# Delta rule: the inverse's products with z and with the z-part of k v made for all chunks at once, and wide norms by GpSimd's power

## Chip, cores and metric

One core of one Trainium2 chip runs one launch. The metric is the device time of that launch in microseconds; the median of three runs of the kernel before is 3610.85 us (3596.32 to 3610.88).

## The reference, cut to what matters

Three layers over 2048 tokens of width 1024: sliding window attention, a gated recurrence (HGRN2), and a hybrid of gated linear attention and the RWKV-7 delta rule, each between norms. What the change touches most is the delta rule, per head of 64 and per token:

```
sa = jnp.einsum('bhvk,bhk->bhv', S, -kk_t)
S = (S * w_t[:, :, None, :]
     + sa[..., None] * (kk_t * a_t)[:, :, None, :]
     + v_t[..., None] * k_t[:, :, None, :])
y = jnp.einsum('bhvk,bhk->bhv', S, r_t)
```

There are 8 such heads. The other touched piece is `lax.rsqrt(mean + eps)` of the norms: per head of 128 in the recurrence and in the linear attention, per head of 64 behind the delta rule.

## The kernel before, in words

The tokens are taken in four phases of 512. Matrix products of the layers (`ch`, `ch_two`, `unit_tok`) run in float32r as three products of 128-row high and low parts: `hth` and `htl` are activations, `wp` weights, `psA` and `psB` the PSUM banks of this main stream. Heads are worked on beside it in float32: `hgrn_head` and `gla_pair` with `gate_out`, and `delta_pair`.

`delta()` walks through the delta rule as one thread: four phases, and in each four pairs of heads, 16 calls of `delta_pair` in all. A pair's 512 tokens are 8 chunks of 64. Phase by phase a pair needs columns `u` that the main stream writes to DRAM. In a pair:
- products of decayed k, b with z and r give the masked blocks `AS`; the part that is to be inverted goes to DRAM (`md`, 4 transfers) and comes back as `Mb` (lines 1775 to 1805);
- 31 pairs of VectorE operations (`pr`, `X`, lines 1839 to 1841) invert 32 by 32 blocks; `X` goes to DRAM (`xd`, 4 transfers) and comes back as `XB` (1844 to 1849); two rounds of 32 by 32 products (`psV`, `psX`) complete the inverse `Xt`, 64 by 64 for each chunk and head;
- `psU` (1826 to 1835) is what z takes from k v, put into the upper half of `VV`, whose lower half is v;
- the recurrence (1885 to 1909) runs over the 8 chunks: `psQ` is the product of z and r with the state `Sbd`; VectorE adds `VV` (`P1`, tile `P`); TensorE multiplies by the inverse (`psQ<-P,Xt`); ScalarE copies the result into `VV`; TensorE makes the state's increment `psSt` and completes the output in `psQ` (`psQ<-VV,AS`); VectorE updates `Sbd`; ScalarE copies the output to `y`;
- norm, gate and a transfer of the pair's output, on which the last layer's out product (`F`) waits.

`rsqrt` (537) makes a norm's factor. For one column a GpSimd power does it; for 4 columns (`gate_out`, 1414: 48 calls) and 8 (`delta_pair`, 1919: 16 calls) VectorE makes it with a bit shift and three Newton steps, 11 operations on tiles `rsi` and `rst` behind the first.

The order of instructions on each engine is written out ahead. `Threads` interleaves the generators by an estimate of time; each instruction is recorded with its cost and what it depends on (`Pace.record`, 261), and `Pace.order` (314) simulates the five queues (the SP queue issues every transfer) and fixes the order in each. While the main stream is on TensorE, side work is let in when it has been ready for 1 us, and then all that is ready together. The last pair is moved ahead in priority (line 1668). `record` takes a DRAM tensor's access as one interval, so the four `xd` writes, which interleave, count as depending on one another in this plan. The planner's price for a GpSimd power is line 243:

```
            return 0.4 + n * 0.165
```

PSUM banks of `delta_pair` come from `psb`, two of them; SBUF buffers from `dbig`, 16.

Of the kernel before, what the change touches and what calls it, by code (L numbers as in the profile page):

```python
# [11 lines left out]
F32 = mybir.dt.float32  # L12
F32R = mybir.dt.float32r
BF16 = mybir.dt.bfloat16
I32 = mybir.dt.int32
AF = mybir.ActivationFunctionType
ALU = mybir.AluOpType
AX = mybir.AxisListType
PSUM = bass.MemoryType.PSUM
DRAM = bass.MemoryType.DRAM  # L20

P = 128
# [122 lines left out]
class Pace:  # L145
# [115 lines left out]
    def record(self, ins, eng, op, outs, ins_, rest, priority):  # L261

        n, deps = len(self.log), set()
        inside = lambda a, b: a[0] >= b[0] and a[1] <= b[1] and a[2] >= b[2] and a[3] <= b[3] and not b[4]
        for x in outs + ins_:
            name = x.tensor.name
            if self.follows.get(name):
                deps.add(self.first[self.follows[name]])
            self.first.setdefault(name, n)
        for x in ins_:  # L270
            key, area = self.area(x)
            w, r = self.uses.setdefault(key, [[], []])
            deps.update(i for a, i in w if x.space == "PSUM" or self.meet(a, area))
            if x.space == "PSUM":
                deps.update(i for _, i in r if self.log[i][1] != eng)
        for x in ins_:
            key, area = self.area(x)
            self.uses[key][1].append((area, n))
        for x in outs:
            key, area = self.area(x)  # L280
            u = self.uses.setdefault(key, [[], []])
            for k in range(2):
                deps.update(i for a, i in u[k] if i != n and (x.space == "PSUM" or self.meet(a, area)))
                u[k][:] = [v for v in u[k] if v[1] == n or not inside(v[0], area)]
            u[0].append((area, n))
        table = next((self.TABLES[f] for f in rest if f in self.TABLES), None) if eng == "act" else None
        mode = None
        if eng == "pe":
            rows, cols = ins_[0].shape[0], math.prod(ins_[0].shape[1:])
            if op == "transpose":  # L290
                cols = P
            mode = *(32 if k <= 32 else 64 if k <= 64 else P for k in (rows, cols)), "r" if ins_[0].dtype == F32R else "t" if op == "transpose" else "f"
        if eng == "dma" and any(s != 1 or k <= 256 for x in (outs[0], ins_[0]) for s, k in x.ap[-1:]):
            self.short.add(n)
        saved, self.table = self.table, table[0] if table else self.table
        cost = self.cost(eng, op, outs, ins_, rest)
        self.table = saved
        self.begin.append(self.at["pe"] if eng == "dma" and self.at["pe"] < 80.0 else 0.0)
        self.log.append((ins, eng, cost, deps, priority, table, mode))
# [191 lines left out]
def rec_stack(ctx: ExitStack, tc: tile.TileContext, A, out, T=2048, layers=(0, 1, 2)):  # L491
    nc = tc.nc
    NPH = T // TQ
    pace = Pace(tc)
    te, ve, se, ge, sy = (pace.engine(e, n) for e, n in (
        (nc.tensor, "pe"), (nc.vector, "dve"), (nc.scalar, "act"), (nc.gpsimd, "pool"), (nc.sync, "dma")))
# [5 lines left out]
    mx = ctx.enter_context(tc.tile_pool(name="mx", bufs=1))  # L502
    turn = Turns(mx, 1, pace)
    sm = Turns(ctx.enter_context(tc.tile_pool(name="sm", bufs=4)), 4, pace)
# [6 lines left out]
    yrow = Buffers(mx, "y", 4, pace)  # L511
    mrg = Buffers(mx, "g", 8, pace)
    big = Buffers(mx, "a", 13, pace)
    dbig = Buffers(mx, "b", 16, pace)
    psd = Buffers(psp, "d", 2, pace)
    psm = Buffers(psp, "m", 4, pace)
    psb = Buffers(psp, "e", 2, pace)

    def need(ev):
        if ev not in done:  # L520
            yield ev

    def bank(pool, name, ahead=0):
        return pool.take([P, TQ], F32, name, ahead=ahead)
# [12 lines left out]
    def rsqrt(dst, src, scale, eps, n):  # L537

        ve.tensor_scalar(dst, src, scale, eps, ALU.mult, ALU.add)
        if n == 1:  # L540
            ge.tensor_tensor(dst, dst, mhalf, ALU.pow)
            return

        i = sm.tile([P, 8], I32, tag="rsi", name="rsi")[:, :n]
        t = sm.tile([P, 8], F32, tag="rst", name="rst")[:, :n]
        y = i.bitcast(F32)
        ve.tensor_scalar(i, dst.bitcast(I32), 1, None, ALU.logical_shift_right)
        ve.tensor_scalar(i, i, -1, 0x5f3759df, ALU.mult, ALU.add)
        for k in range(3):
            ve.tensor_tensor(t, y, dst, ALU.mult)  # L550
            ve.scalar_tensor_tensor(t, t, -0.5, y, ALU.mult, ALU.mult)
            ve.scalar_tensor_tensor(y if k < 2 else dst, t, 1.5, y, ALU.add, ALU.mult)


    def w_ch(w, *cols):
# [145 lines left out]
    H2 = [slice(0, 64), slice(64, 128)]  # L701
# [22 lines left out]
    def row_stat(x, name, rstd=None):  # L724
        ss = sm.tile([P, 1], F32, tag="ss" + name, name="ss" + name)
        se.activation(out=junk, in_=x, func=AF.Square, accum_out=ss)
        if rstd is None:
            rstd = sm.tile([P, 1], F32, tag="rstd" + name, name="rstd" + name)
        rsqrt(rstd, ss, 1.0 / D, EPS, 1)
        return rstd  # L730
# [160 lines left out]
    ident = cst.tile([P, P], F32, name="ident")  # L891
    junk = cst.tile([P, D], BF16, name="junk")
    mhalf = cst.tile([P, 1], F32, name="mhalf")
# [779 lines left out]
    def delta_pair(ph, hp, wa):  # L1673
# [4 lines left out]
        def new(name, shape=(P, TQ), dt=F32):  # L1678
            return dbig.take(list(shape), dt, name)
# [5 lines left out]
        for n in (hp, 4 + hp, 8 + hp):  # L1685
            yield from need(("u", n, ph))
            t = yield from new("u")
            sy.dma_start(out=t, in_=ud[n, ph])
            src.append(t)
        r, k, v = src  # L1690
# [5 lines left out]
        ps = yield from bank(psb, "psW")  # L1696
# [5 lines left out]
        ps = yield from bank(psb, "psAa")  # L1702
# [14 lines left out]
        ps = yield from bank(psb, "psN")  # L1717
# [19 lines left out]
        ZR, BK = [], []  # L1737
# [19 lines left out]
        AS = [[None, None], [None, None]]  # L1757
        for h in range(2):
# [4 lines left out]
            for c in range(4):  # L1763
                for n in range(2):
                    te.matmul(pn[n][:, P * c:P * c + P], lhsT=BK[h][H2[n], c].rearrange("p f t -> p (f t)"),
                              rhs=ZR[h][H2[n], c].rearrange("p f t -> p (f t)"), start=True, stop=True)
# [24 lines left out]
        ps = yield from bank(psb, "psVT")  # L1791
# [4 lines left out]
        VV = []  # L1796
# [10 lines left out]
        ps = yield from bank(psb, "psBo")  # L1807
# [6 lines left out]
        BKt = []  # L1814
        for h in range(2):
            ps = yield from bank(psb, "psBK")
# [6 lines left out]
            psb.give(ps)  # L1823
        dbig.give(*BKh)

        for h in range(2):
            ps = yield from bank(psb, "psU")
            for c in range(4):
                for n in range(2):
                    te.matmul(ps[0:64, P * c + 64 * n:P * c + 64 * n + 64], lhsT=AS[n][h][64:128, 0, c],  # L1830
                              rhs=VV[h][64:128, c, 64 * n:64 * n + 64], start=True, stop=True)
                yield
            yield
            se.copy(VV[h][0:64].rearrange("p c d -> p (c d)"), ps[0:64])
            psb.give(ps)
# [14 lines left out]
        Xt = []  # L1850
# [10 lines left out]
        ps = yield from bank(psb, "psV2")  # L1861
        for m in range(16):
            c, n = divmod(m, 2)
# [6 lines left out]
        ps = yield from bank(psb, "psX")  # L1870
# [6 lines left out]
            se.copy(Xt[h][0:32, :, 32:64], ps[0:32, 256 * h:256 * h + 256].rearrange("p (m t) -> p m t", m=8))  # L1877
        psb.give(ps)

        gate = yield from new("gate")  # L1880
        yield from need(("u", 13 + hp, ph))
        sy.dma_start(out=gate, in_=ud[13 + hp, ph])
        y = yield from new("y", (P, 4, P))
        yield
        for c in range(8):
            h, cc = divmod(c, 4)
            pq = yield from bank(psb, "psQ")
            te.matmul(pq[:, 0:P], lhsT=ZR[h][:, cc].rearrange("p f t -> p (f t)"), rhs=Sbd, start=True, stop=True)
            yield
            P1 = sm.tile([64, P], F32, tag="P1", bufs=1, name="P1")  # L1890
            ve.tensor_tensor(P1, pq[0:64, 0:P], VV[h][0:64, cc], ALU.add)
            yield
            for n in range(2):
                te.matmul(pq[0:64, P + 64 * n:P + 64 * n + 64], lhsT=Xt[h][:, 2 * cc + n], rhs=P1[:, H2[n]], start=True, stop=True)
            yield
            se.copy(VV[h][0:64, cc], pq[0:64, P:2 * P])
            yield
            pst = yield from bank(psb, "psSt")
            for n in range(2):
                te.matmul(pst[H2[n], 0:64], lhsT=BKt[h][:, cc, n], rhs=VV[h][:, cc, H2[n]], start=True, stop=True)  # L1900
            for n in range(2):
                te.matmul(pq[64:128, H2[n]], lhsT=AS[n][h][:, 1, cc], rhs=VV[h][:, cc, H2[n]], start=False, stop=True, skip_group_check=True)
            yield
            for n in range(2):
                ve.scalar_tensor_tensor(Sbd[H2[n], H2[n]], Sbd[H2[n], H2[n]], WC[H2[n], c], pst[H2[n], 0:64], ALU.mult, ALU.add)
            psb.give(pst)
            yield
            se.copy(y[H2[c % 2], c // 2], pq[64:128, 0:P])
            psb.give(pq)
        dbig.give(*ZR, *VV, *Xt, *BKt, *AS[0], *AS[1])  # L1910

        mv = sm.tile([P, 8, 2], F32, tag="mv", name="mv")
        for i in range(4):
# [12 lines left out]
        ps = yield from bank(psb, "psYT")  # L1926
# [26 lines left out]
    for i, (kind, ph) in enumerate(order):  # L1953
        head, body, tail, chains, n = build[kind](i, ph, seq)
# [88 lines left out]
```

## Time and profile before

| | |
|---|---|
| median of three runs | 3610.85 us |
| the profiled execution | 3609.73 us |
| its span, first to last instruction | 3607.9 us |
| TensorE matmul busy | 3418.6 us, 95% |
| VectorE busy | 2395.9 us, 66% |
| ScalarE busy | 1298.1 us, 36% |
| GpSimd busy | 438.6 us, 12% |
| transfers in flight, share of 16 engines | 55% |
| mean granted TensorE clock | 0.976 |

The profiled execution lies 1.9 us above its span and 1.1 us under the median. Every recorded operation has the same source line (the helper that emits it), so rows are told apart by their tiles. A float32 product appears as two matmul instructions, a transpose and a float32r product as one.

### The profile page before, as it was taken

Reading aid. Unit: us, or ns where it says so; the run is one execution under the profiler, and the core shown is the slowest. Engines: PE = TensorE matmul, PEld = TensorE weight load, DVE = VectorE, ACT = ScalarE, POOL = GpSimd, SP = SyncE. Lnnn points to the kernel's source line nnn. Section 1 sums busy time; section 2 is a strip of 40 time slices with the busy share of each in tenths; the row PEclk is TensorE's granted clock in tenths of the full one; section 3 lists DMA queues with packets and bytes.
Section 4 is the critical chain, followed back from the end, with each engine's and each line's share of the span. In section 5 each row is a group of like instructions: output and inputs, shape, how many; then the busy total and the mean of one; then the engine's idle time right before and its main releaser. Section 6 shows DMA issues by size and latency. Waiting matters only on the chain.

```text
span 3607.9 us, 76010 instructions
## 1 busy us (share of the span) xinstructions
PE 3418.6 (95%) x30488; PEld 2929.9 (81%) x30488; DVE 2395.9 (66%) x6735; ACT 1298.1 (36%) x3379; POOL 438.6 (12%) x649
## 2 busy tenths in 40 slices
PE   4999999999999999999999999999999999999997
PEld 4788888888878788878787787888888787888886
DVE  4777666567675876986747758665766766566574
ACT  3655433345433232454222324422232332333232
POOL 2321135410150000000000002300000000011000
PEclk8999999999999999999999999999999999999998
DMA  7666567755586344444754345675344366455663
GB/s 192 184 205 220 172 228 237 235 178 192 208 276 215 128 130 147 148 164 166 246 200 133 123 142 166 238 257 172 122 141 156 110 239 236 155 176 164 233 226 128
DMA packets 351105, 666.35 MB, mean 185 GB/s; under 512 B 164640, under 2 KB 246560, under 8 KB 298016
## 3 DMA queue, kind: packets, MB, share of 16 engines
q1 hardware_dynamic: 350752, 661.49, 55.1%
q8 instruction: 240, 3.93, 0.4%
q14 instruction: 113, 0.93, 0.1%
HBM read 494.42 MB, written 166.99 MB: 183 GB/s over the span
## 4 chain that ended last, share of the span: by engine, by line
PE 68%; DVE 21%; DMA 5%; ACT 3%; issue 2%; SPq 1%; POOL 0%; DVEq 0%; ACTq 0%; POOLq 0%
PE psA L431 29%; PE psB L431 18%; DVE pr L431 4%; PE psO L431 4%; PE psQ L431 3%; DVE X L431 3%; PE psL L431 2%; PE psPT L431 2%; PE psS L431 2%; DVE y L431 1%; SPq L431 1%; DVE AS L431 1%; DMA wp<-wk 1%; PE psT L431 1%; PE psKV L431 1%
## 5 line engine op out<-in xcount | busy, mean ns | idle before, releaser
L431 PE MATMUL psA<-hth,wp 128*128 128x512 f32 (+1 forms) x5120 | 1477.1, 367 | 65.3 <-ACT qs L431 27.4
L431 PEld LDWEIGHTS psA<-hth,wp 128*128 128x128 f32 x5120 | 914.7, 192 | 221.1 <-ACT qs L431 27.8
L431 PE MATMUL psA<-htl,wp 128*128 128x512 f32 (+1 forms) x2560 | 934.9, 366 | 0.0
L431 PE MATMUL psB<-wp,mgh 128*128 128x256 f32 x3072 | 579.5, 286 | 9.2 <-DVE y L431 3.4
L431 PEld LDWEIGHTS psA<-htl,wp 128*128 128x128 f32 x2560 | 490.8, 192 | 68.8 <-issue 5.3
L431 PEld LDWEIGHTS psB<-wp,mgh 128*128 128x128 f32 x3072 | 480.8, 190 | 20.5 <-issue 4.9
L431 POOL TENSOR_TENSOR wp<-wf,wp 128x256 fp32r<-128x256 f32 x412 | 344.5, 868 | 897.2 <-ACT wp L431 890.1
L431 PE MATMUL psB<-wp,mgl 128*128 128x256 f32 x1536 | 440.5, 287 | 3.4 <-DVE mgl L431 3.4
L431 PE MATMUL psB<-wp,hth 128*128 128x256 f32 x1536 | 300.3, 291 | 4.6 <-DMA wp<-wk 2.3
L431 PEld LDWEIGHTS psB<-wp,mgl 128*128 128x128 f32 x1536 | 291.1, 190 | 7.8 <-DVE mgl L431 5.1
L431 PEld LDWEIGHTS psB<-wp,hth 128*128 128x128 f32 x1536 | 245.5, 193 | 10.5 <-DMA wp<-wk 2.8
L431 PE MATMUL psB<-wp,htl 128*128 128x256 f32 x768 | 222.8, 290 | 0.0
L431 DVE TENSOR_TENSOR pr<-X,Mb 128x16 f32<-128x16 f32 (+30 forms) x496 | 207.1, 417 | 10.9
L431 DVE TENSOR_TENSOR y<-psB,y 128x256 f32<-128x256 f32 x256 | 97.2, 418 | 123.3 <-PE psB L431 122.6
L431 DVE SCALAR_TENSOR_TENSOR Sbd<-Sbd,WC,psSt 64x64 f32<-64x64 f32 x256 | 71.4, 279 | 161.0 <-PE psSt L431 157.8
L431 POOL MEMSET Xt<- 32x256 f32 x32 | 9.7, 304 | 1197.1 <-PE psM L431 891.7
L431 DVE TENSOR_REDUCE X<-pr 128x8 f32<-128x16 f32 (+30 forms) x496 | 146.0, 294 | 11.2
L431 ACT ACTIVATE junk<-y 128x1024 bf16<-128x1024 f32 (+1 forms) x128 | 94.4, 737 | 161.6 <-DVE y L431 149.4
L431 PEld LDWEIGHTS psB<-wp,htl 128*128 128x128 f32 x768 | 148.5, 193 | 3.0 <-issue 1.5
L431 ACT CAST wp<-wf 128x1024 fp32r<-128x1024 f32 x103 | 108.0, 1049 | 112.6 <-PE psB L431 49.4
L431 ACT ACTIVATE S<-S,nm 128x257 f32<-128x257 f32 (+1 forms) x256 | 126.8, 498 | 56.9 <-DVE nm L431 54.3
L431 ACT COPY VV<-psQ 64x128 f32<-64x128 f32 x128 | 33.1, 259 | 244.3 <-PE psQ L431 242.6
(283 smaller groups left out, 5457.2 us busy)
## 6 DMA issues: line engine op xcount, KB each, us to landing
wp<-wk SPq DMA_DIRECT2D x309, 1024.0 KB, 5.1
wk<-wp SPq DMA_DIRECT2D x103, 1024.0 KB, 5.3
xin<-x SPq DMA_DIRECT2D x48, 512.0 KB, 5.1
wf<-in_rec_w_in_dram SPq DMA_DIRECT2D x32, 512.0 KB, 6.8
x<-y SPq DMA_DIRECT2D x32, 512.0 KB, 3.6
wf<-in_w_in_dram SPq DMA_DIRECT2D x29, 512.0 KB, 6.6
ud<-um SPq DMA_DIRECT2D x52, 256.0 KB, 4.2
u<-ud SPq DMA_DIRECT2D x48, 256.0 KB, 3.4
```

The source lines that it names most:

```text
L431: r = f(*a, **k)
```

## The change

- In `delta_pair`, z of each chunk is transposed on TensorE by a product with the identity (`Zt`, two banks, a ScalarE copy each), ahead of `psU`.
- When `Xt` is complete, 16 products of 64 by 64 (`psXZ`) put the inverse times z where z stood in `ZR`, and 16 more (`psXU`, two banks) put the inverse times what z takes from k v where that stood in `VV`; ScalarE copies, two for `psXZ` and one for each bank of `psXU`.
- In the recurrence the product with `Xt` and ScalarE's copy are gone: VectorE's addition writes `VV` itself.
- `dbig` has 18 buffers in place of 16.
- `rsqrt` is a GpSimd power for any number of columns.
- In the planner, a write to a DRAM tensor depends on earlier reads of it alone, no longer on earlier writes.

```
-            for k in range(2):
+            for k in range(1 if x.space == "DRAM" else 0, 2):
                 deps.update(i for a, i in u[k] if i != n and (x.space == "PSUM" or self.meet(a, area)))
-                u[k][:] = [v for v in u[k] if v[1] == n or not inside(v[0], area)]
+                if x.space != "DRAM":
+                    u[k][:] = [v for v in u[k] if v[1] == n or not inside(v[0], area)]
...
-    dbig = Buffers(mx, "b", 16, pace)
+    dbig = Buffers(mx, "b", 18, pace)
...
         ve.tensor_scalar(dst, src, scale, eps, ALU.mult, ALU.add)
-        if n == 1:
-            ge.tensor_tensor(dst, dst, mhalf, ALU.pow)
-            return
-
-        i = sm.tile([P, 8], I32, tag="rsi", name="rsi")[:, :n]
-        t = sm.tile([P, 8], F32, tag="rst", name="rst")[:, :n]
-        y = i.bitcast(F32)
-        ve.tensor_scalar(i, dst.bitcast(I32), 1, None, ALU.logical_shift_right)
-        ve.tensor_scalar(i, i, -1, 0x5f3759df, ALU.mult, ALU.add)
-        for k in range(3):
-            ve.tensor_tensor(t, y, dst, ALU.mult)
-            ve.scalar_tensor_tensor(t, t, -0.5, y, ALU.mult, ALU.mult)
-            ve.scalar_tensor_tensor(y if k < 2 else dst, t, 1.5, y, ALU.add, ALU.mult)
+        ge.tensor_tensor(dst, dst, mhalf.to_broadcast([P, n]), ALU.pow)
...
+        Zt = []
+        for h in range(2):
+            ps = yield from bank(psb, "psZ")
+            for c in range(4):
+                te.matmul(ps[0:64, P * c:P * c + P], lhsT=ZR[h][:, c, 0], rhs=ident, start=True, stop=True)
+            Zt.append((yield from new("Zt", (64, 4, P))))
+            yield
+            se.copy(Zt[h].rearrange("p c d -> p (c d)"), ps[0:64])
+            psb.give(ps)
...
+        ps = yield from bank(psb, "psXZ")
+        for c in range(8):
+            h, cc = divmod(c, 4)
+            for n in range(2):
+                te.matmul(ps[H2[n], 64 * c:64 * c + 64], lhsT=Zt[h][:, cc, H2[n]], rhs=Xt[h][:, 2 * cc + n], start=True, stop=True)
+        yield
+        for h in range(2):
+            se.copy(ZR[h][:, :, 0], ps[:, 256 * h:256 * h + 256].rearrange("p (c t) -> p c t", c=4))
+        psb.give(ps)
+        dbig.give(*Zt)
+        for h in range(2):
+            ps = yield from bank(psb, "psXU")
+            for cc in range(4):
+                for n in range(2):
+                    te.matmul(ps[0:64, P * cc + 64 * n:P * cc + 64 * n + 64], lhsT=Xt[h][:, 2 * cc + n], rhs=VV[h][0:64, cc, H2[n]], start=True, stop=True)
+            yield
+            se.copy(VV[h][0:64].rearrange("p c d -> p (c d)"), ps[0:64])
+            psb.give(ps)
+        dbig.give(*Xt)
...
-            P1 = sm.tile([64, P], F32, tag="P1", bufs=1, name="P1")
-            ve.tensor_tensor(P1, pq[0:64, 0:P], VV[h][0:64, cc], ALU.add)
-            yield
-            for n in range(2):
-                te.matmul(pq[0:64, P + 64 * n:P + 64 * n + 64], lhsT=Xt[h][:, 2 * cc + n], rhs=P1[:, H2[n]], start=True, stop=True)
-            yield
-            se.copy(VV[h][0:64, cc], pq[0:64, P:2 * P])
+            ve.tensor_tensor(VV[h][0:64, cc], pq[0:64, 0:P], VV[h][0:64, cc], ALU.add)
```

## Rows read from the trace of the kernel before

**Rows 1.** The page, part 1: busy time, share of the span, instructions.
```profile
PE 3418.6 (95%) x30488; PEld 2929.9 (81%) x30488; DVE 2395.9 (66%) x6735; ACT 1298.1 (36%) x3379; POOL 438.6 (12%) x649
```

**Rows 2.** Busy time by stretch; columns: length, busy by engine (instructions), clock, DMA share, GB/s.
```profile
3000.00:3545.00 545.00, 518.98 (x4127) 456.57 (x4126) 336.01 (x953) 169.43 (x460) 36.73 (x71) 0.97 0.59 197
3545.00:3575.00 30.00, 15.90 (x106) 11.68 (x104) 13.84 (x56) 4.52 (x14) 0.00 (x0) 0.60 0.10 36
```

**Rows 3.** TensorE's waits from 1050 to 3545 us: total us, times, longest.
```profile
PE psMT L431 <- ACT mt L431: 11.0, 12, 2.2
```

**Rows 4.** Groups of TensorE instructions by shape: count, busy us, mean ns, idle before.
```profile
L431 PE MATMUL psQ<-P,Xt 64*64 64x64 f32 x512 | 57.2, 233 | 2.4 <-DVE P L431 2.3
```

**Rows 5.** Timeline of TensorE at 1104 us: start, length, instruction.
```profile
1103.89 0.28 PE L431 MATMUL psA<-htl,wp 128*128 128x256 f32 x1
1104.10 0.44 PE L431 MATMUL psQ<-P,Xt 64*64 64x64 f32 x4
...
1104.81 0.28 PE L431 MATMUL psA<-htl,wp 128*128 128x256 f32 x1
...
1105.17 0.28 PE L431 MATMUL psA<-htl,wp 128*128 128x256 f32 x1
```

**Rows 6.** Timeline of TensorE at 2645 us, where two side groups follow each other.
```profile
2645.49 0.44 PE L431 MATMUL psQ<-P,Xt 64*64 64x64 f32 x4
2645.86 0.46 PE L431 MATMUL psL<-QR,KL 128*32 128x32 f32 x32
```

**Rows 7.** Timeline of TensorE at 3462 us, around `psU`.
```profile
3461.93 0.27 PE L431 MATMUL psB<-wp,mgl 128*128 128x256 f32 x1
3462.14 2.08 PE L431 MATMUL psU<-VV,AS 64*64 64x64 f32 x32
...
3464.48 0.28 PE L431 MATMUL psB<-wp,mgl 128*128 128x256 f32 x1
```

**Rows 8.** Timeline of TensorE at 1108 us, around the product with the state.
```profile
1108.25 0.28 PE L431 MATMUL psA<-htl,wp 128*128 128x256 f32 x1
1108.37 0.38 PE L431 MATMUL psQ<-Sbd,ZR 128*128 128x128 f32 x2
...
1108.83 0.29 PE L431 MATMUL psA<-htl,wp 128*128 128x256 f32 x1
```

**Rows 9.** Timeline of TensorE from 3533 us, last pair, `psQ` instructions alone kept.
```profile
3533.41 0.49 PE L431 MATMUL psQ<-Sbd,ZR 128*128 128x128 f32 x2
...
3535.51 0.44 PE L431 MATMUL psQ<-P,Xt 64*64 64x64 f32 x4
...
3537.80 0.40 PE L431 MATMUL psQ<-VV,AS 128*64 128x64 f32 x4
...
3539.78 0.39 PE L431 MATMUL psQ<-Sbd,ZR 128*128 128x128 f32 x2
```

**Rows 10.** Timeline of all engines from 3553 us, last pair's fifth and sixth chunk.
```profile
3553.63 0.28 DVE L431 TENSOR_TENSOR P<-psQ,VV 64x128 f32<-64x128 f32 x1
...
3555.07 0.48 PE L431 MATMUL psSt<-VV,BKt 128*64 128x64 f32 x4 [0.35 <-ACT VV L431]
...
3557.07 0.28 DVE L431 TENSOR_TENSOR P<-psQ,VV 64x128 f32<-64x128 f32 x1 [0.89 <-PE psQ L431]
```

**Rows 11.** Busy time over the span of the instructions that touch `rsi`, VectorE only.
```profile
0.00:3608.00 3608.00, 114.62 (x704) 0.98 0.56 185
```

**Rows 12.** Timeline of all engines at 12 us: two powers and a VectorE operation.
```profile
12.13 0.55 POOL L431 TENSOR_TENSOR rstdi<-rstdi,mhalf 128x1 f32<-128x1 f32 x1 [2.35 <-DVE rstdi L431]
...
12.76 1.28 DVE L431 SCALAR_TENSOR_TENSOR xin<-xin,rstdi,bci 128x1024 f32<-128x1024 f32 x1
12.91 1.54 POOL L431 TENSOR_TENSOR rstdi<-rstdi,mhalf 128x1 f32<-128x1 f32 x1 [0.23 <-DVE rstdi L431]
```

**Rows 13.** Timeline of the SP queue at 2721 us: issues of transfers.
```profile
2721.50 1.72 SPq L431 DMA_DIRECT2D xd<-X  x4
...
2729.57 0.32 SPq L431 DMA_DIRECT2D XB<-xd  x1
```

More of the change, by code (lines that the diff above doesn't have):

```diff
@@ L1889, in delta_pair @@
             yield
-            P1 = sm.tile([64, P], F32, tag="P1", bufs=1, name="P1")
-            ve.tensor_tensor(P1, pq[0:64, 0:P], VV[h][0:64, cc], ALU.add)
-            yield
-            for n in range(2):
-                te.matmul(pq[0:64, P + 64 * n:P + 64 * n + 64], lhsT=Xt[h][:, 2 * cc + n], rhs=P1[:, H2[n]], start=True, stop=True)
-            yield
-            se.copy(VV[h][0:64, cc], pq[0:64, P:2 * P])
+            ve.tensor_tensor(VV[h][0:64, cc], pq[0:64, 0:P], VV[h][0:64, cc], ALU.add)
             yield
@@ L1909, in delta_pair @@
             psb.give(pq)
-        dbig.give(*ZR, *VV, *Xt, *BKt, *AS[0], *AS[1])
+        dbig.give(*ZR, *VV, *BKt, *AS[0], *AS[1])
         mv = sm.tile([P, 8, 2], F32, tag="mv", name="mv")
```

## Prediction

> **What bounds the kernel now.** I read the page first, then the stretches, the waits of TensorE, and the timelines of single visits. TensorE is busy 95% of the span, no other engine over 66% [rows 1], so what counts first is how long its queue is, and only then how long a pair of the delta rule takes. From 3000 to 3545 us TensorE is idle 26 of 545 us; the one stretch after the start where it runs dry is 3545 to 3575 us, with 15.9 us busy of 30 at a granted clock of 0.60, between the levels of 1.2 and 2.4 GHz [rows 2]. There the last pair's recurrence stands alone, as the timeline of rows 10 shows: each step waits for the one before it on another engine.
>
> So the change has two places with different limits. Before 3545 us a shorter chain buys nothing by itself and each TensorE instruction costs its time. In the last 30 us it is the other way round.
>
> **Part 1, TensorE work removed.** The products with `Xt` are 512 instructions [rows 4], four for each of 128 chunks. Where such a visit stands alone in the main stream, the `htl` product behind it starts 0.92 us after the one ahead of it, against 0.36 us for an undisturbed period of three products [rows 5]: 0.56 us for the visit. Of this 0.25 us is the two products (see part 2) and 0.31 us the change to side work and back. Where other side work follows at once, 0.37 us passes until that starts [rows 6]. So 128 visits are worth 47 to 72 us; I take the middle, 60 us, as both kinds are common.
>
> **Part 2, TensorE work added**, per pair:
> - `psXU`: 16 products of the very shape of `psU`. A `psU` visit costs 3464.48 - 3461.93 = 2.55 us less 0.36, that is 2.19 us [rows 7]; less 0.31 for the visit, 1.88 us, or 0.12 us a product (two are the 0.25 above).
> - `psZ`: 8 products with 128 columns on the right. The state's product has those columns and costs 0.58 - 0.36 = 0.22 us [rows 8]; the weights here are half as wide, which might halve it: 0.9 to 1.76 us. I take 1.76, the same columns being streamed.
> - `psXZ`: 16 products like `psU`, but with outputs alternating between the halves of the bank, which may overlap: 0.94 to 1.88 us. I take 1.4 us, the middle.
> - five banks mean three to five visits, 0.12 us each if shared, 0.31 if alone: 0.4 to 1.55 us, taken as 0.95 us.
>
> That is 6.0 us a pair, 96 us for 16; bounds 4.1 and 7.1 us, 66 and 113 us. The two unknown shares go together: if all visits are alone, 72 us go and 6.6 x 16 = 105 come, net +33; if all are shared, 47 go and 5.44 x 16 = 87 come, net +40. I take +36 us, with 1.8 us less a pair if both overlaps work: +7 us at the low end, +48 us at the high. Some of it falls ahead of one of TensorE's waits, which then shrinks; with 5% idle I count 4 us for this. **Net +32 us.**
>
> **Part 3, ScalarE and VectorE in the pair.** ScalarE loses 8 copies of 64x128 and gains six larger ones, at 36% load: nothing, as its idle time covers it; without cover it would be some 1 us a pair, 16 us. VectorE's addition stays as it is, with another target. The new waits: ScalarE waits for `psZ`, `psXZ` and `psXU`, and behind it stand copies that free the main stream's banks; `psQ` of the first chunk now waits for the copy of `psXZ`, where before it ran as soon as the state was there. On the path of one pair this adds one visit, one copy and a hand-over on each side, some 5 us, hidden except in the last pair (part 5).
>
> **Part 4, norms.** 64 calls lose 11 VectorE operations each, 704 in 114.6 us [rows 11]. GpSimd gains 64 powers. One column takes 0.55 us [rows 12]; four and eight columns cost between that (35 us in all) and proportionally more (2.2 and 4.4 us, 176 us in all). The planner's formula, 1.06 and 1.72 us, fits the one-column row (0.565) and gives 78 us; I take it. GpSimd is 12% busy [rows 1]. A power beside a long VectorE operation took 1.54 us in place of 0.55 [rows 12], so the relief of VectorE is smaller than the 114.6 us. TensorE waits for norms little: 11.0 us for `psMT` [rows 3], of which the norm is only one cause. **-8 us**, from 0 to -20: the low end adds other waits on VectorE.
>
> The Trainium skill, SBUF — State Buffer, section on who interferes with whom, says that a VectorE instruction with two SBUF inputs and a GpSimd instruction that reads SBUF exclude one another for the whole instruction. The stretched power agrees: its partner has two SBUF tensors as inputs, ends at 14.04 us, and the power ends 0.41 us later [rows 12]. What it would do at worst is the third rival.
>
> **Part 5, the end.** While the main stream runs, a chunk of the last pair takes 6.37 us, of which 2.29 us pass from the product with `Xt` to the one that uses its result [rows 9]; standing alone, 3.44 us from addition to addition, of which 1.44 us from the addition to `psSt` [rows 10], where the addition's own 0.28 and a hand-over of about 0.1 remain: 1.06 us saved. So a pair's eight chunks shorten by 8.5 us (all alone) to 18 us (all within the main stream), less the 5 us of part 3. Four pairs follow each other in the last phase, 13 to 50 us in sum. The main stream's own lengthening there is 4 x 2 us. So the last pair should be over before the main stream runs dry. What can be won is the 30 us less the work in it, 15.9 us at 0.60, about 10 us at full clock: 20 us. The main stream's order is fixed in advance and may not fill the gap fully, so **-17 us**, from -5 to -20.
>
> **Part 6, plan and buffers.** The four `xd` transfers are issued back to back in 1.72 us in one pair, and `XB` 8.07 us after the first [rows 13], so the dependence that the planner saw is not a wait on the chip. Without it `XB` can be placed some microseconds earlier, a gain on the pair's path that only the last phase shows, already covered by the cap in part 5. The number of transfers stays, but each queue is ordered anew, the SP queue included; a transfer that is put behind a late one costs or spares a wait of a few microseconds. I count 0, from -8 to +8. Two more buffers hold `Zt`: 0.
>
> **Sum.** +32 - 8 - 17 = +7 us on the profiled 3609.7 us: 3617 us, 6 us above the median. A measurement here can tell about 0.5%, 18 us, from no change, so that is no change.
>
> **Rivals.**
> 1. *Slower: TensorE takes all of it.* Nothing is absorbed (+36 to +40), the norms give nothing, and the last phase, with a longer TensorE queue, still ends in a lone recurrence, now about five chunks x 1.06 us shorter (five of 3.44 us with the norm and the gate fill the 30): +40 - 5 = +35, 3645 us. For it: 95% busy, and a removed product reappears as at least one added. Against: 30 us of near idleness at the end. It decides when the net is over 35 us and the end gives under 17. Chance 0.24.
> 2. *Faster: the visits, not the products, are the cost.* `psXZ` and `psZ` overlap (+7 us net), the VectorE relief gives 15 us and the end 17: -25 us, 3585 us. For it: 0.31 of 0.56 us of a lone visit are no product. Against: rows 7 show no overlap for this shape. Chance 0.23.
> 3. *Slower: powers and VectorE get in each other's way.* Each of 64 powers waits 1 us as in rows 12, and half of them hold up what TensorE waits for: 20 to 30 us added to the sum, about 3640 us. For it: the stretched power. Against: before, powers are stretched seldom and GpSimd is near idle. By the Trainium skill's rule above, whichever began first holds the other, so VectorE could lose too. Chance 0.06.
>
> The change not doing what it says is no rival: the diff removes the product from the loop.
>
> **How the numbers follow.** The forecast, within 0.5%, has 0.47; slower is rivals 1 and 3, 0.30; faster is rival 2, 0.23. The range takes rival 2's time as its low end and reaches a little past rival 1's, 3585 to 3648 us. The likeliest case alone spans 3593 to 3629 us.
>
> **What would show it.** Right: `psQ<-P,Xt` gone; 16 x 16 `psZ` instructions near 0.11 us apart, `psXU` at 2 us for 32; TensorE's undisturbed stretches longer by about 2 us a pair; `rsi` gone, powers near 1.1 and 1.7 us; the 3545 to 3575 stretch filled, with its clock near 1. Wrong: the lone recurrence still there (rival 1), `psXZ` under 1 us (rival 2), powers of 2 us and longer, with `mt` or `y` waiting for GpSimd (rival 3).

## The result, and the profile after

The changed kernel takes 3560.66 us in the median of four runs (3556.53 to 3567.48), the kernel before 3604.28 us beside it: a ratio of 0.9882, 95% interval 0.9850 to 0.9913. That is 1.2% faster, where +7 us and no change were forecast, and 24 us below the range. The profiled execution took 3562.99 us, its span is 3561.2 us.

The page, part 1, of the kernel after [rows 1]:

```profile
PE 3408.9 (96%) x31256; PEld 2945.3 (83%) x31256; DVE 2316.4 (65%) x6031; ACT 1314.8 (37%) x3349; POOL 523.6 (15%) x713
```

TensorE has 768 instructions more (512 gone, 1280 new) and still is 96% busy; VectorE lost the 704 of the norms, GpSimd gained 64. Busy time by stretch of the kernel after, columns as in [rows 2]:

```profile
3000.00:3500.00 500.00, 490.68 (x4161) 436.11 (x4161) 314.11 (x823) 172.40 (x452) 50.55 (x79) 0.99 0.59 198
3500.00:3530.00 30.00, 29.44 (x239) 28.62 (x238) 18.63 (x44) 6.41 (x16) 2.73 (x4) 1.00 0.84 283
3530.00:3561.00 31.00, 20.87 (x175) 20.67 (x173) 11.98 (x28) 8.16 (x32) 2.17 (x4) 0.91 0.30 121
```

The 30 us in which TensorE ran half empty at a granted clock of 0.60 are gone: the stretch at the same distance from the end is filled at 1.00. And the last phase ahead of it has 9 us idle in 500, where it had 26 in 545. Behind the lone recurrence, the kernel before ended in a stretch much like the last one here, at a clock of 0.86 where 0.91 is granted now:

```profile
3575.00:3608.00 33.00, 22.59 (x174) 22.37 (x174) 12.64 (x29) 8.17 (x32) 2.17 (x4) 0.86 0.25 96
```

What became of the last pair is seen from what TensorE still had to do behind its transpose `psYT`. Groups of TensorE instructions from there to the end, of the kernel before:

```profile
L431 PE MATMUL psB<-wp,mgh 128*128 128x256 f32 x116 | 22.3, 295 | 3.0 <-ACT mgh L431 3.0
L431 PE MATMUL psB<-wp,mgl 128*128 128x256 f32 x58 | 16.8, 292 | 0.0
```

and of the kernel after:

```profile
L432 PE MATMUL psB<-wp,mgh 128*128 128x256 f32 x318 | 57.9, 282 | 0.1
L432 PE MATMUL psB<-wp,mgl 128*128 128x256 f32 x160 | 45.3, 284 | 0.5 <-DVE mgl L432 0.5
```

174 products were all that was left before, those that need this pair; now 478 are left, so TensorE has other work while the pair is being finished.

**The new products.** Groups by shape, kernel after:

```profile
L432 PE MATMUL psXU<-VV,Xt 64*64 64x64 f32 x512 | 35.7, 220 | 0.0
L432 PE MATMUL psU<-VV,AS 64*64 64x64 f32 x512 | 33.4, 220 | 0.0
L432 PE MATMUL psZ<-ident,ZR 128*64 128x128 f32 x256 | 31.8, 276 | 0.0
L432 PE MATMUL psXZ<-Xt,Zt 64*64 64x64 f32 x512 | 18.4, 221 | 0.0
```

`psXZ` has the count and shape of `psU` and takes 18.4 us against 33.4, though one instruction takes the same 0.22 us: the outputs of `psXZ` alternate between the two halves of a bank. That this is the reason is shown by `e12_overlapped` below. Together the three new groups are busy 85.9 us; the 57.2 us of [rows 4] are gone. Timeline of TensorE in the tenth pair, side groups kept:

```profile
2571.95 1.15 PE L432 MATMUL psXZ<-Xt,Zt 64*64 64x64 f32 x32
2572.93 1.09 PE L432 MATMUL psXU<-VV,Xt 64*64 64x64 f32 x16
...
2574.34 1.14 PE L432 MATMUL psXU<-VV,Xt 64*64 64x64 f32 x16
2575.41 0.49 PE L432 MATMUL psQ<-Sbd,ZR 128*128 128x128 f32 x2
```

`psXZ` and the first half of `psXU` share a visit, and so do the second half and the first `psQ`. A chunk in the last pair while the main stream runs, timeline of TensorE [rows 9]:

```profile
3454.29 0.49 PE L432 MATMUL psQ<-Sbd,ZR 128*128 128x128 f32 x2
...
3456.39 0.34 PE L432 MATMUL psSt<-VV,BKt 128*64 128x64 f32 x4
...
3458.54 0.39 PE L432 MATMUL psQ<-Sbd,ZR 128*128 128x128 f32 x2
```

4.25 us where it was 6.37. The SP queue, in the pair of [rows 13]:

```profile
2685.61 1.72 SPq L432 DMA_DIRECT2D xd<-X  x4
...
2688.63 0.32 SPq L432 DMA_DIRECT2D XB<-xd  x1
```

`XB` follows 3.02 us after `xd`, not 8.07. That pair had the shortest such distance of all 16 before: there it is 8.07 to 20.86 us, 12.4 in the mean, and now 2.94 to 6.65 us, 4.4 in the mean; over the four pairs of the last phase 32 us less in sum. The powers of the norms, all instructions on the constant -0.5 (ns min/median/max):

```profile
L432 POOL TENSOR_TENSOR hrs<-hrs,mhalf x48: 1002/1015/1981, 506.6 to 3369.6; 128x4 f32<-128x4 f32 x48
...
L432 POOL TENSOR_TENSOR grs<-grs,mhalf x16: 1947/2008/2312, 1138.4 to 3487.2; 128x8 f32<-128x8 f32 x16
```

and the wait of [rows 3], in the waits of TensorE of the kernel after:

```profile
PE psMT L432 <- ACT mt L432: 3.9, 4, 1.9
```

### The profile page after: what moved, and what is told of

It reads as the page before. It is cut to its first block, busy times and chain, and to the rows that moved or that the text cites. A ratio compares the mean times of both kernels' runs of the same rounds, so it can differ in the third digit from the quotient of the medians.

```text
span 3561.2 us, 77069 instructions
## 1 busy us (share of the span) xinstructions
PE 3408.9 (96%) x31256; PEld 2945.3 (83%) x31256; DVE 2316.4 (65%) x6031; ACT 1314.8 (37%) x3349; POOL 523.6 (15%) x713
## 4 chain that ended last, share of the span: by engine, by line
PE 73%; DVE 17%; DMA 5%; ACT 2%; issue 2%; SPq 1%; POOL 0%; DVEq 0%; POOLq 0%; ACTq 0%
PE psA L432 31%; PE psB L432 20%; PE psO L432 4%; DVE pr L432 4%; DVE X L432 3%; PE psQ L432 2%; PE psS L432 2%; PE psPT L432 2%; PE psL L432 1%; DMA wp<-wk 1%; SPq L432 1%; PE psT L432 1%; PE psU L432 1%; PE psSt L432 1%; PE psXU L432 1%
## 5 line engine op out<-in xcount | busy, mean ns | idle before, releaser
L432 PEld LDWEIGHTS psB<-wp,hth 128*128 128x128 f32 x1536 | 244.4, 192 | 12.7 <-issue 3.2
L432 DVE TENSOR_TENSOR QR<-QR,T 128x256 f32<-128x256 f32 x192 | 85.5, 446 | 67.9 <-PE psL L432 57.6
L432 DVE CUSTOM_DVE_ANT_0 S<-psS,amask,sink 128x256 f32<-128x256 f32 (+1 forms) x256 | 113.0, 469 | 15.9 <-PE psS L432 14.8
```

The costliest lines, as they stand in the source:

```text
L432: r = f(*a, **k)
```

## The experiments

Three edits came together, so they were first taken alone. Each ratio is to the kernel before on the same chip, with its 95% interval. Line numbers and rows are as in the kernel they are of.

**Products alone** (`e1_products_only`): the kernel after with the old `record` and the old `rsqrt`. The two added buffers go with the products here and in every run below; what they are worth by themselves is not shown.

```
-            for k in range(1 if x.space == "DRAM" else 0, 2):
+            for k in range(2):
...
-        ge.tensor_tensor(dst, dst, mhalf.to_broadcast([P, n]), ALU.pow)
+        if n == 1:
+            ge.tensor_tensor(dst, dst, mhalf, ALU.pow)
+            return
...
+        for k in range(3):
+            ve.tensor_tensor(t, y, dst, ALU.mult)
```

> The moved products and the two buffers alone; norms and plan as before. Theory A (the gain lies at the end, where the delta rule is through before the main stream runs dry; until about 3300 us the moved products break even): 3570 to 3585 us, 20 to 35 us under before, the last pair's transpose psYT some 50 us earlier than before's 3571 us, and TensorE's products 22 to 36 us longer until 3300 us unless fewer turns pay for them. Theory B (the plan without false DRAM dependences shortens a pair): no more than 10 us under before. Theory C (the norms relieve VectorE, and that is the gain): as before or up to 30 us slower, since TensorE's queue is longer.

Measured: 3639.53 us, 1.0105 (1.0088 to 1.0123), slower by 38 us. Neither theory A nor B stands; C comes nearest, and the first two parts of the prediction too. The end, busy time by stretch:

```profile
3575.00:3608.00 33.00, 23.61 (x206) 21.40 (x205) 18.79 (x68) 4.89 (x12) 0.00 (x0) 0.87 0.35 128
3608.00:3642.00 34.00, 23.20 (x174) 23.00 (x174) 12.50 (x29) 8.15 (x32) 2.16 (x4) 0.80 0.25 93
```

The lone recurrence is still there, better filled (23.6 of 33 us), with the 174 products behind it.

**Norms alone** (`e2_norms_only`): only `rsqrt` is exchanged.

> The GpSimd power for 4 and 8 columns alone. Theory A: 5 to 20 us under before (fewer stalls of TensorE behind VectorE), the lone recurrence at the end still there. Theory C: 30 us or more under before. Theory B: no change within 5 us.

Measured: 3595.63 us, 0.9985 (0.9975 to 0.9994), 5.6 us faster, the low end of theory A; B, no change within 5 us, is missed narrowly, and C falls.

**Plan alone** (`e3_plan_only`): only `record` is exchanged.

> The planner's DRAM rule alone. Theory A: within 8 us of before; XB issued some 5 us sooner after xd, pairs some 5 us shorter, the lone recurrence at the end shorter by up to 15 us. Theory B: 20 us or more under before. Theory C: no change within 5 us.

Measured: 3587.04 us, 0.9966 (0.9952 to 0.9981), 14 us faster, between A and B. `XB` follows `xd` after 4.4 us in the mean of the 16 pairs, as in the whole change.

**Priority in place of products** (`e4_last_phase_ahead`):

```
-                if ph == NPH - 1 and hp == 3:
+                if ph == NPH - 1 and hp == 0:
```

> The kernel before with its whole last phase of the delta rule moved ahead in priority, where only the last pair was; no computation changed. Theory A: part of the end's gain comes without moving any product: 5 to 25 us under before, the last pair's psYT earlier than 3571 us and less idle TensorE in the last 60 us; if a pair's length is set by its own waits and not by its place in the queues, no more than 5 us. Theories B and C: no change within 5 us.

Measured: 3619.32 us, 1.0054 (1.0040 to 1.0068), slower by 18 us. A miss. The pairs of the last phase took longer, not shorter: the last transpose came 600.8 us behind the start of the last phase's first pair, where it had been 583.1 (table below). Why is open.

By themselves the edits sum to 38 - 5.6 - 14 = +18 us, but together they give -42. Each was therefore taken out of the whole, and the order was shaken by `HOLD`, the planner's constant for how long side work must have been ready before the main stream is left; it changes the order alone and nothing that is computed.

**Without the norms** (`e5_no_norms`) and **without the plan** (`e6_no_plan`): the kernel after with the old `rsqrt`, and with the old `record`.

> The changed kernel with the norms on VectorE again (products, buffers and plan stay). The products alone were 38 us slower, norms alone 5 and the plan alone 13 us faster, yet all three together 42 us faster: 62 us are in the combination. Theory I (the plan and the moved products act together: once the recurrence is short, what a pair waits for is the transfers that the old plan puts late): close to the whole change, 3560 to 3575 us. Theory N (it is the norms that act with the products): 3600 us or more. Theory L (every edit reorders all queues, and an order by itself is worth some 20 us either way): anywhere between 3560 and 3640 us, and the next runs with a neutral constant of the planner changed move by 10 us or more.

> The changed kernel with the old plan of DRAM writes (products, buffers and norms stay). Theory I: most of the gain is gone, 3610 to 3640 us. Theory N: close to the whole change, 3560 to 3575 us. Theory L: anywhere between 3560 and 3640 us.

Measured: 3593.62 us, 0.9981 (0.9971 to 0.9990), and 3593.12 us, 0.9978 (0.9968 to 0.9987). Each is worth some 33 us in the whole (35 by the ratios), so neither I nor N stands for the time. But the ends differ. Without the norms the end is filled as in the change, and the last transpose comes 69 us before the end; without the plan the lone recurrence is there again, better filled than in the kernel before, and the transpose comes 37 us before the end. Busy time by stretch, start of the last phase's first pair and last transpose of `e5_no_norms`:

```profile
3530.00:3560.00 30.00, 29.43 (x239) 28.63 (x239) 17.72 (x43) 6.44 (x17) 2.73 (x4) 1.00 0.83 282
L432 PE MATMUL psW<-wa,up x2: 589/641/693, 3006.9 to 3007.5; 64*128 64x512 f32 x2
L432 PE MATMUL psYT<-ident,y x64: 270/273/329, 1145.6 to 3522.9; 128*128 128x128 f32 x64
```

and the same of `e6_no_plan`:

```profile
3525.00:3557.00 32.00, 23.20 (x199) 20.98 (x199) 17.26 (x55) 4.89 (x12) 2.02 (x1) 0.90 0.29 105
L431 PE MATMUL psW<-wa,up x2: 590/642/694, 2986.0 to 2986.6; 64*128 64x512 f32 x2
L431 PE MATMUL psYT<-ident,y x64: 270/272/472, 1151.3 to 3552.7; 128*128 128x128 f32 x64
```

**The order shaken** (`e7_products_hold09`, `e8_after_hold09`, then `e9_before_hold09`):

```
-    HOLD = 1.0
+    HOLD = 0.9
```

> The products alone, as in the first experiment, with the planner's HOLD (how long side work must have been ready before the main stream is left) at 0.9 us in place of 1.0: nothing is computed otherwise, only the order differs. Theories I and N: within 8 us of 3639.5 us. Theory L: 10 us or more away from it.

> The whole change with HOLD at 0.9 us. Theories I and N: within 8 us of the changed kernel's 3560.7 us. Theory L: 10 us or more above it, since the change as it stands would be a lucky order.

> The kernel before with HOLD at 0.9 us. HOLD moved the products alone by 22 us and the whole change by 12. Theory L (an order by itself is worth 10 to 20 us): 10 us or more from before, either way. Theories I and N: within 8 us of before.

Measured: products alone 3617.68 us, 1.0052 (1.0035 to 1.0068), 22 us better than with 1.0 (19 by the ratios); the change 3573.09 us, 0.9931 (0.9910 to 0.9953), 12 us worse (18 by the ratios); the kernel before 3610.98 us, 1.0039 (1.0026 to 1.0053), 13 us worse. Theory L stands in all three: one order against another can be worth 10 to 20 us, so a single pair of kernels does not tell what an edit of that size is worth.

**Norms and plan without the products** (`e13_norms_and_plan`):

> Norms and plan without the moved products. If effects add: 5.6 + 14 = 20 us under before, 3581 us. Theory T (the end is a threshold: only with products and plan together is the last pair over before the main stream runs dry): the sum, 3575 to 3590 us, and the lone recurrence still at the end, with 174 main-stream products behind the last pair's transpose as before. If it comes near 3561 us the moved products give nothing.

Measured: 3568.39 us, 0.9920 (0.9898 to 0.9942): 30 of the 42 us, lower than any expectation but the last clause's. Its end, busy time by stretch:

```profile
3500.00:3545.00 45.00, 34.69 (x288) 30.88 (x288) 22.58 (x68) 6.96 (x20) 2.02 (x1) 0.84 0.44 150
3545.00:3578.00 33.00, 22.38 (x174) 22.16 (x174) 12.51 (x29) 8.17 (x32) 2.16 (x4) 0.86 0.25 96
```

TensorE idles 10 us of 45 and its clock falls to 0.84: the lone recurrence is shorter, but still there, with 174 products behind it.

**Three orders of each** (`e14` to `e17`, HOLD at 1.1 or 0.9), run because the products' part was still open:

> The kernel before with HOLD at 1.1 us. Theory L: 3590 to 3620 us, 5 to 15 us from the run at 1.0.

> The whole change with HOLD at 1.1 us. Theory T (products with the plan fill the end, whatever the order): 3555 to 3580 us, more than 400 main-stream products still to come behind the last pair's transpose. If the order at 1.0 was only lucky: over 3580 us.

> Norms and plan without the products, HOLD at 0.9 us. Theory T: 3570 to 3595 us, with the lone recurrence at the end (174 products behind the last transpose). If the products give nothing, the same mean as the whole change, 3560 to 3573 us.

> Norms and plan without the products, HOLD at 1.1 us. Theory T: 3570 to 3595 us. If the products give nothing: 3555 to 3580 us, as for the whole change at 1.1.

Measured: 3601.25 us, 1.0001 (0.9991 to 1.0012); 3557.27 us, 0.9880 (0.9857 to 0.9903); 3576.06 us, 0.9931 (0.9906 to 0.9957); 3565.83 us, 0.9907 (0.9881 to 0.9934). At each of the three settings the change is 1.1 or 1.2% under the kernel before at the same setting, so its gain is no luck of one order. Three expectations missed. At 1.1 the kernel before did not move (5 to 15 us were expected). At 1.1 the change has 192 products behind the last transpose, not over 400, though its end is filled all the same (30.0 of the 30 us from 3480 us on). And at 1.1 norms and plan took 3565.83 us, below theory T's 3570 and within the range named for the case that the products give nothing.

That case is not ruled out for the whole time: beside norms and plan the products gain 14, 0 and 10 us by the ratios at 1.0, 0.9 and 1.1, and the intervals overlap at each. Norms and plan alone give 25 to 33 us against the kernel before at 1.0.

All orders together, one profiled execution each (`psW` is the start of the last phase's first pair, which the main stream sets by writing `u`, from the instructions on `psW`; the next column is the start of the last `psYT` less that; the last is the span less that):

| kernel | HOLD | ratio | `psW` at, us | from there to the last transpose, us | from there to the end, us |
|---|---|---|---|---|---|
| before | 1.0 / 0.9 / 1.1 | 1 / 1.0039 / 1.0001 | 2988.5 / 2986.6 / 2979.6 | 583.1 / 584.7 / 582.7 | 619.4 / 622.1 / 620.1 |
| products | 1.0 / 0.9 | 1.0105 / 1.0052 | 3025.1 / 3009.4 | 579.4 / 568.7 | 616.4 / 605.2 |
| norms | 1.0 | 0.9985 | 2979.8 | 577.2 | 614.6 |
| plan | 1.0 | 0.9966 | 2986.6 | 569.0 | 605.5 |
| products, norms (`e6`) | 1.0 | 0.9978 | 2986.0 | 566.7 | 603.7 |
| products, plan (`e5`) | 1.0 | 0.9981 | 3006.9 | 516.0 | 585.4 |
| norms, plan | 1.0 / 0.9 / 1.1 | 0.9920 / 0.9931 / 0.9907 | 2975.6 / 2970.3 / 2959.9 | 565.9 / 562.5 / 562.9 | 602.1 / 598.8 / 599.6 |
| all three | 1.0 / 0.9 / 1.1 | 0.9882 / 0.9931 / 0.9880 | 2985.2 / 2992.8 / 2973.2 | 506.5 / 514.2 / 543.6 | 576.0 / 580.9 / 579.6 |

The rows of the transpose and of `psW` (from 2900 to 3040 us) on which two of these entries rest, of the kernel before:

```profile
L431 PE MATMUL psYT<-ident,y x64: 270/272/472, 1168.6 to 3571.6; 128*128 128x128 f32 x64
L431 PE MATMUL psW<-wa,up x2: 589/641/693, 2988.5 to 2989.0; 64*128 64x512 f32 x2
```

and of the kernel after:

```profile
L432 PE MATMUL psYT<-ident,y x64: 270/272/328, 1141.9 to 3491.7; 128*128 128x128 f32 x64
L432 PE MATMUL psW<-wa,up x2: 589/641/693, 2985.2 to 2985.7; 64*128 64x512 f32 x2
```

The last transpose comes 80 us earlier, `psW` 3 us. Busy time by stretch up to `psW` and from there on, of the kernel before:

```profile
0.00:2988.50 2988.50, 2850.01 (x26018) 2431.03 (x26018) 2023.18 (x5679) 1110.93 (x2861) 399.76 (x574) 0.98 0.56 184
2988.50:3607.90 619.40, 568.60 (x4471) 498.92 (x4470) 372.69 (x1057) 187.17 (x518) 38.89 (x75) 0.95 0.55 187
```

and of the kernel after:

```profile
0.00:2985.20 2985.20, 2853.19 (x26596) 2448.90 (x26596) 1958.51 (x5106) 1122.47 (x2837) 468.03 (x626) 0.98 0.56 185
2985.20:3561.20 576.00, 555.70 (x4663) 496.44 (x4662) 357.90 (x925) 192.32 (x513) 55.53 (x87) 0.99 0.59 201
```

Ahead of `psW` TensorE executes 578 instructions more, and 12 pairs x 48 are 576, so `psW` parts the same work in both. The last column moves by 3 us or less with the order in the kernel before and by 5 us at most in the whole change, but by 11 us with the products alone; `psW` itself moves by 9 to 20 us, so the order's luck is mostly in the three phases ahead. Read down:
- The products cost, until `psW`, 36.6 and 22.8 us without the other edits, 6.2 beside the norms, 20.3 beside the plan, and 9.6, 22.5 and 13.3 us beside both (same HOLD): 19 us in the mean of seven.
- From there to the end they give back 26.1, 17.9 and 20.0 us beside norms and plan and 20.1 beside the plan; without the plan 3.0, 16.9 and, with the norms, 10.9.
- The plan gives 12.5 to 13.9 us there without the products, and 31.0 and 27.7 with them. Up to the last transpose this is plainest: products alone take 4 us off, the plan alone 14, both together 67. Why each needs the other is not shown.
- The norms give 3.4 to 12.7 us there. Until `psW` they give 8.7 us alone, 11.0 beside the plan, 39.1 beside the products and 21.7 beside both, the plan 4.2 us at most but for 18.2 beside the products alone, whose order was unlucky.

**TensorE's work taken away** (`e11_transposed_z`, `e12_overlapped`). If TensorE's queue is the bound up to the end, work taken from it is time.

```
-                te.matmul(ps[0:64, P * c:P * c + P], lhsT=ZR[h][:, c, 0], rhs=ident, start=True, stop=True)
+                te.transpose(ps[0:64, P * c:P * c + P], ZR[h][:, c, 0], ident)
```

> The whole change with z transposed by TensorE's transpose, one instruction, in place of a product with the identity, two. TensorE loses 128 instructions of 0.107 us, 13.7 us. Theory Q (until the end TensorE's queue is the bound, so work taken from it is time): 8 to 18 us under the change, 3543 to 3553 us, with the order's noise of some 12 us on top. If the pair's chain is the bound: no more than 3 us.

Measured: 3548.19 us, 0.9864 (0.9846 to 0.9881), 12.5 us under the change by the medians, as theory Q has it, but 6 us by the ratios, with overlapping intervals; one order's luck is as large, so this run alone does not settle it. Its time from `psW` to the end is 590.5 us, 14.5 more than the change's: the last column, too, can move with the order. The second also lets `psU` and `psXU` alternate, in one bank each; the new code of `psXU`, with `psU` alike:

```
...
+        ps = yield from bank(psb, "psXU")
+        for c in range(8):
+            h, cc = divmod(c, 4)
+            for n in range(2):
+                te.matmul(ps[H2[n], 64 * c:64 * c + 64], lhsT=Xt[h][:, 2 * cc + n], rhs=VV[h][0:64, cc, H2[n]], start=True, stop=True)
+        yield
+        for h in range(2):
+            for n in range(2):
+                se.copy(VV[h][0:64, :, H2[n]], ps[H2[n], 256 * h:256 * h + 256].rearrange("p (c t) -> p c t", c=4))
+        psb.give(ps)
...
```

> As the run before, and psU and psXU also write their outputs alternately into the two halves of a bank, one bank each in place of two, as psXZ does. In the changed kernel psXZ took 15.7 us of TensorE's time for the same 256 products for which psU takes 32.2 and psXU 33.5, so 34 us more go, and up to 32 visits of 0.3 us. Theory Q: 25 to 45 us under the run with the transpose alone, 3500 to 3530 us. If the chain is the bound: no more than 5 us.

Measured: 3512.67 us, 0.9762 (0.9745 to 0.9778), 35.5 us under the run with the transpose alone and 86 under before. Groups by shape:

```profile
L432 PE MATMUL psXZ<-Xt,Zt 64*64 64x64 f32 x512 | 19.2, 227 | 0.0
L432 PE MATMUL psXU<-VV,Xt 64*64 64x64 f32 x512 | 18.4, 224 | 0.0
L432 PE MATMUL psU<-VV,AS 64*64 64x64 f32 x512 | 18.4, 221 | 0.0
L432 PE MATMUL psZ<-ident,ZR 128*64 128x128 f32 x128 | 16.9, 273 | 0.0
```

`psU` and `psXU` now take what `psXZ` takes, 32 us less than in the change, and the time fell by 35 us, more than any order above has moved a kernel (22 us). This version beats both kernels.

## Why the prediction was wrong

**What failed.** Part 5's cap on the end, and part 6, which put the plan at 0 as "already covered by the cap in part 5". The cap took the end as the 30 us of the lone recurrence less the work in them, 20 us, and let products and plan share 17. From `psW` to the end 43, 41 and 41 us went, in three orders, with the longer TensorE queue of four pairs already in it. The step looked at one gap only. Of the 43.4 us, 30.5 are idle time of TensorE: some 14 in that gap, and 17 among the last phase's other 26 idle us of [rows 2], which were taken as given. The other 12.9 us are busy time, though 192 instructions are new there: the recurrence had a granted clock of 0.60, and the mean from `psW` on rose from 0.95 to 0.99.

The plan's 0 failed with it. `XB` comes 8 us sooner in the mean of the 16 pairs, with the plan alone (4.4 us behind `xd`, as in `e5_no_norms`) and not without it (12.3 us in `e6_no_plan`). The row that part 6 read, 8.07 us, is the shortest of all pairs. Alone the plan gives 14 us; in the whole it gives 28 us behind `psW`. The products and the plan together bring the last pair ahead of the main stream, with 478 products left in place of 174, and they do so without the norms (`e5_no_norms`), while without the plan the lone recurrence stays. Each shortens the pairs (`XB` 8 us sooner, a chunk 2 us shorter); that together they take off more than the sum of both is measured, and the reason for that is open.

Laid beside the sum: with 12 of 16 pairs ahead of `psW`, it has 24 - 6 = +18 us until `psW` and 8 - 2 - 17 = -11 us behind it; in the profiled executions these are -3 and -43 us. So the end was off by 32 us and the part ahead of it by 21. There the products cost less beside the other edits (9.6 us) and norms and plan gave more (12.9 us), but one order's luck is as large.

**Parts 1 and 2** said +36 us for 16 pairs, that is 27 for the 12 ahead of `psW`, or 24 with the stalls that absorb some. Measured there: 19 us in the mean of seven comparisons, from 6 to 37. Right in size. In detail `psXZ` was overestimated, 22 us against 18.4 measured; `psXU` (30) and `psZ` (28) were under, with 35.7 and 31.8 us of busy time, which counts the run-out of each group's last instruction.

**The sum of products alone**, +32 - 17 = +15 us, stands against +38 and, at the other HOLD, 1.0052 against 1.0039, that is +5 us, which is not clear of noise. The sign is right at 1.0; of the two orders, that one was the unlucky one. The forecast gain of 17 us at the end was not had by the products alone in the first (3 us) and was in the second (16.9 us).

**Part 4** priced the powers well: 1.02 and 2.01 us where 1.06 and 1.72 were taken. The 8 us given for the norms were 5.6 alone. In the whole they are worth more: 31 us between the profiled executions of `e5_no_norms` and of the change, 22 ahead of `psW`, where the sum had 6, and 9 behind it. How much of the 22 is the norms' and how much the order's was not parted.

**Rivals.** Rival 1's price, +35 us, holds for the products alone at 1.0 (+38), where its condition (a lone recurrence still at the end) holds too; at 0.9 they are 17 us over the kernel before at 1.0. Rival 2 had the sign, and its overlap of `psXZ` is real; that of `psZ`, whose outputs all go to one half, is not: 31.8 us for 128 products of two instructions. Its time was not reached by way of it: norms and plan alone give 30 of the 42 us. Rival 3 did not come about: single powers were stretched, to 1.98 and 2.31 us at most, but the medians lie 1 to 3% above the shortest ones (1.00 and 1.95 us), and TensorE's wait for `psMT` fell from 11.0 to 3.9 us.

**Not settled**: why the norms are worth 9 to 39 us ahead of `psW`, in which the order's luck of 9 to 20 us is contained; why products and plan need each other; and whether the products, in this layout, gain anything over norms and plan alone (0 to 14 us), as what they give back at the end they cost ahead of it.

## What to carry to other kernels

Where a fixed order of queues is computed from a cost model, shake a neutral constant of it and compare means: here that alone is worth 0 to 22 us, as much as most single edits. When a side chain ends a kernel, price each shortening of the chain by how far it moves the chain's end ahead of the work that can cover it, and count every idle stretch that this clears, not only the last. Read a wait over all its occurrences before pricing it: the one pair read here had the shortest of 16. And on a full TensorE, how small products are laid out decides: the same 256 float32 products cost half when their outputs alternate between the halves of a bank.

## What the runs showed of the hardware that was not expected

- Alternating output halves: 256 products of 64 by 64 by 64 take 18.4 us against 33.4 to 35.7 us, and where two such groups got it, the kernel was 35.5 us shorter; the two groups take 32 us less of TensorE than in the change.
- A GpSimd power costs 0.55, 1.02 and 2.01 us for 1, 4 and 8 columns (medians).
